# A state-space stage between gate products: the small products of a batch put in one run, VectorE's order written as a list, and weight tables multiplied out of PSUM

## The chip, the cores and the metric

The kernel runs on one core of a Trainium2 chip. The core has TensorE (PE, with a separate line PEld for loading weights), VectorE (DVE), ScalarE (ACT), GpSimd (POOL) and SyncE (SP), which issues transfers. Each engine takes its instructions in one fixed order and waits at the first one whose inputs or buffers are not ready. SBUF is the memory that the engines work from. PSUM, in eight banks, takes what PE writes; DVE and ACT read and write it too.

The metric is the time of one execution on the device, in microseconds (us). The kernel before took 1144.9 us as the median of three runs (1141.12, 1144.90 and 1145.05).

## The reference, cut to what matters

The program is a trunk of two layers on 1024 time steps of width 1024, all in float32. Layer 0 projects the input once and feeds three things: a diagonal complex state-space layer, retention, and two gates; layer 1 is a convolution module.

```python
proj = h @ w_in                          # u_s5, g_s5, q, k, v, g_ret
# state-space layer: 64 groups of 16 channels, 64 complex states each
bu  = einsum('tbgh,gnh->tbgn', u, bb)    # bb: complex, from a, dt, b
x_t = lb * x_{t-1} + bu_t                # lb = exp(dt * a), complex, per state
y_t = re(einsum('tbgn,ghn->tbgh', x_t, c)) + d * u_t
y_s5  = glu(gelu(y)) * silu(g_s5)
y_ret = retention(q, k, v) * silu(g_ret)
x = x + concat(y_s5, y_ret) @ w_out
```

The change touches the recurrence (bu, x_t, y_t) and the order in which it stands between the products for `g_s5` and `g_ret`.

## The kernel before, in words

Every large product is computed three times over 128x512 tiles, with the high and low parts of both operands: high weight by high input, high weight by low input, low weight by high input (`mm3`, L200 to L202). A weight block of 128x1024 is loaded as `wf`, cast by ACT to its high part `wh` (L189) and the rest `wl = wf - wh` is made by DVE or POOL (L190); for the gate blocks g9 to g23 it is DVE.

The stage concerned is the second part of `layer0_front`. It makes the 16 gate blocks g8 to g23. A gate block is two halves of 24 matmuls (`mm_g`), and each half is scaled by DVE out of its PSUM bank (`gt = mm_g * R`, L393), then passed through Silu by ACT (L394). Between the gate blocks stand the eight batches B = 0 to 7 of the state-space layer, 128 channels in each, one batch to every two gate blocks. A batch works on 8 time steps at once:

- POOL multiplies out tables from powers of `lb`: `Mr`, `Mi` (input side), `Tc`, `Ts` (a rotation that makes the recurrence real), `W3` (output side), in L766 to L768.
- `W2` holds the input weights. For B = 0 and 1 it is `Mr`, `Mi` turned by PE (L857) and copied by ACT (L859). From B = 2 on DVE makes it by six products (L806 to L811) from tables `PT`, `BT` that transfers lay out in SBUF.
- PE: `v` = `U` x `W2` into two PSUM banks (L868). PE also makes the direct response of the first 8 steps, `kp` (L902, L903); ACT copies 112 of its columns to `Kg` (L905), and DVE adds the term `d` in the other 16 (L906). PE turns `Kg` (L908, the tile is `kt`), ACT copies it out, a transfer stores it in `k_d` and another (L915) reads it back as the banded table `Wd`, which ACT copies to `W1` (L917).
- DVE, on the two banks of `v`: a rotation (L876 to L881), two scans (L883), the rotation back (L890 to L893) and the states `S` (L894, L895).
- PE: `y` = `U` x `W1` (L932) + `S` x `W3` (L938), which ACT copies out (L942).

`v`, `kp`, `kt`, `y` and, for B = 0 and 1, the turned `W2` share five PSUM banks in turn (`ps_aux`). The gate blocks have three of their own. A scheduler sets the order on every engine, from a simulated timeline; `chained` fixes the order of a group of instructions among themselves only, and `issue_after` puts one behind another. `y` of a batch is written in the code behind the gate block that follows the next batch's `v`.

Of the kernel before, what the change touches and what calls it, by code (L numbers as in the profile page):

```python
# [11 lines left out]
F32 = mybir.dt.float32  # L12
# [3 lines left out]
ALU = mybir.AluOpType  # L16
# [3 lines left out]
P = 128  # L20
# [18 lines left out]
LANES = 2  # L39

# [30 lines left out]
class Trunk:  # L71
# [148 lines left out]
    def run(self):  # L220
# [31 lines left out]
        with ExitStack() as mid:  # L252
            self.mid = self.pool("mid", 1, stack=mid)
            self.ps_aux = self.pool("ps_aux", 5, PSUM, stack=mid)
            with ExitStack() as st:
                self.layer0_front(st)
            with ExitStack() as st:
                self.retention(st)
        with ExitStack() as st:
            self.layer0_back_and_layer1(st)  # L260


    def layer0_front(self, st):
# [3 lines left out]
        early = ExitStack()  # L267
# [145 lines left out]
        self.s5_tab, self.s5_back, self.s5_last = {}, {}, None  # L413
        self.s5_turned()
        self.s5_tables(0)
# [353 lines left out]

    def s5_turned(self):  # L770
# [20 lines left out]
    def s5_w2(self, B):  # L791

        nc, v = self.nc, self.nc.vector
        (ptr, pti), (btr, bti) = ([self.big(f"{n}{c}_{B}", f"{n}{c}", 1) for c in "ri"] for n in ("PT", "BT"))
        dp, db = self.pt_d, self.bt_d

        with self.tc.issue_after(self.u_load.ins):
            for c, (pt, bt) in enumerate(((ptr, btr), (pti, bti))):
                nc.sync.dma_start(pt[:].rearrange("p q n -> p (q n)"),
                                  bass.AP(tensor=dp.tensor, offset=dp.offset + (c * 2 * P + 4 * B) * P,  # L800
                                          ap=[[32 * P, 8], [0, 16], [1, 4 * P]]))
                nc.sync.dma_start(bt[:].rearrange("p q n -> p (q n)"),
                                  bass.AP(tensor=db.tensor, offset=db.offset + (c * 4 * P + 4 * B) * P,
                                          ap=[[0, 8], [32 * P, 16], [1, 4 * P]]))
        w2r, w2i = (self.big(f"W2{nm}_{B}", f"W2{nm}", 1) for nm in "ri")
        v.tensor_tensor(w2r[:], ptr[:], btr[:], op=ALU.mult)  # L806
        v.tensor_tensor(w2i[:], ptr[:], bti[:], op=ALU.mult)
        v.tensor_tensor(ptr[:], pti[:], bti[:], op=ALU.mult)
        v.tensor_tensor(pti[:], pti[:], btr[:], op=ALU.mult)
        v.tensor_tensor(w2r[:], w2r[:], ptr[:], op=ALU.subtract)  # L810
        v.tensor_tensor(w2i[:], w2i[:], pti[:], op=ALU.add)  # L811
        return [w2r, w2i]

    def s5_tables(self, B):
# [25 lines left out]
        self.s5_tab[B] = Mr, Mi, W3, Tc, Ts, R8, self.s5_w2(B) if B > 1 else None  # L840

    def s5_states(self, B):
# [11 lines left out]
        for nm, M in (("r", Mr), ("i", Mi)) if first else ():  # L854
            ps = self.bank(f"w2{nm}_{B}")
# [7 lines left out]
        for c in range(2):  # L863
            ps = self.bank(f"v{c}_{B}")
            for q in range(4):
                for g2 in range(2):
                    r = slice(64 * g2, 64 * g2 + 64)
                    nc.tensor.matmul(ps[r, q * P:(q + 1) * P], W2[c][:, q, r], U[:, 2 * q + g2, :],  # L868
                                     start=True, stop=True)
            V.append(ps)  # L870
        fl = lambda t: t[:].rearrange("p q n -> p (q n)")
# [25 lines left out]


        kp = self.bank(f"kp_{B}")
        for q in range(4):  # L900
            o = kp[q * 32:(q + 1) * 32, :P]
            nc.tensor.matmul(o, self.cbr[:, q0 + q, :], Mr[:, q, :], start=True, stop=False)  # L902
            nc.tensor.matmul(o, self.cbni[:, q0 + q, :], Mi[:, q, :], start=False, stop=True)  # L903
        Kg = w.tile([P, P], F32, name=f"Kg_{B}", tag="Kg", bufs=1)
        nc.scalar.copy(Kg[:, 16:], kp[:, 16:P])  # L905
        v.tensor_tensor(Kg[:, :16], kp[:, :16], self.dd[:, B, :], op=ALU.add)  # L906
        kp = self.bank(f"kt_{B}")
        nc.tensor.transpose(kp[:, :P], Kg[:], self.ident[:])  # L908
        Kt = w.tile([P, P], F32, name=f"Kt_{B}", tag="Kg", bufs=1)
        nc.scalar.copy(Kt[:], kp[:, :P])  # L910

        nc.sync.dma_start(self.k_d[B, 112:], Kt[:])
        Wd = w.tile([P, 8, P], F32, name=f"Wd_{B}", tag="yb", bufs=1)
        kd = self.k_d[B]
        nc.sync.dma_start(Wd[:], bass.AP(tensor=kd.tensor, offset=kd.offset, ap=[[P, P], [16 * P, 8], [1, P]]))  # L915
        W1 = w.tile([P, 8, P], F32, name=f"W1_{B}", tag="W1", bufs=1)
        nc.scalar.copy(W1[:].rearrange("p g (i h) -> p i g h", i=8), Wd[:].rearrange("p i (g h) -> p i g h", g=8))  # L917
        self.s5_back[B] = U, W1, W3, S

    def s5_out(self, B):  # L920
# [5 lines left out]
        ps = [self.bank(f"y{g2}_{B}") for g2 in range(2)]  # L926
# [13 lines left out]
        self.chained(products())  # L940
        for g2 in range(2):
            nc.scalar.copy(yb[:].rearrange("p (q g) m -> p q g m", g=2)[:, :, g2, :],  # L942
# [984 lines left out]
```

## Time and profile before

| what | value |
| --- | --- |
| three runs | 1141.12, 1144.90, 1145.05 us; median 1144.9 |
| the profiled execution, its own time | 1149.41 us |
| its span, from the first instruction to the last | 1147.6 us |
| PE busy | 1125.1 us (98%), 6286 instructions |
| PEld busy | 984.8 us (86%) |
| DVE busy | 850.0 us (74%) |
| ACT busy | 489.0 us (43%) |
| POOL busy | 654.7 us (57%) |
| transfers | 261.45 MB, 228 GB/s in the mean |
| the stage of the eight batches | from about 95 to 323 us of the span |

A row of the timeline gives the start in us from the beginning of the span, the duration in us, the engine, the line, the operation, what it writes and from what, the shape, and a count. The idle time ahead of it stands in square brackets with what ended it. Matmuls overlap one another: the distance between two starts tells what one costs. A row of the waits gives the engine, the instruction that waited and the one that released it; then the idle time, how often, and the mean. A row of the groups gives busy time and mean ns, and behind a bar the idle time just before them. A row of the windows gives its stretch, the length, the busy time of PE, PEld, DVE, ACT and POOL with the number of instructions, the granted clock of PE (1.00 is full speed), the busy share of the DMA engines and GB/s.

### The profile page before, as it was taken

The page shows a single profiled execution, that of the slowest core. Times are in us where ns is not written, and L with a number is a line of the kernel's source. Part 1 is how long each engine was busy: PE and PEld are TensorE (multiplying, and loading weights), DVE is VectorE, ACT ScalarE, POOL GpSimd, SP SyncE. Part 2 cuts the span into 40 slices and gives each one's busy share as a digit, 9 for nine tenths or more (in the row PEclk, how much of TensorE's full clock was granted, in tenths as well). Part 3 has the DMA queues.
Part 4 walks back from the last instruction along what each step waited for, and adds up shares of the span by engine and source line. Part 5 has one row for each costly group of instructions (what it writes and reads, how often), then busy time and mean ns, then how long its engine had stood idle before and what let it go on. Part 6 is the DMA issues. An engine that isn't in the chain of part 4 may idle for free.

```text
span 1147.6 us, 17204 instructions
## 1 busy us (share of the span) xinstructions
PE 1125.1 (98%) x6286; PEld 984.8 (86%) x6286; DVE 850.0 (74%) x1464; ACT 489.0 (43%) x719; POOL 654.7 (57%) x448
## 2 busy tenths in 40 slices
PE   9999989999999999999999999999999999999897
PEld 7888878888888888989887888888888888888787
DVE  6975778887417569486669522599999899999844
ACT  6423222232223231323436423545545676444673
POOL 2059999998236355232575111589544568677563
PEclk9999999999999999999999999999999999999999
DMA  9344345555378766859998988665778655367865
GB/s 353 110 135 153 120 151 175 194 186 179 133 259 278 265 215 193 284 185 333 386 361 299 318 297 283 189 234 203 250 246 297 239 178 172 121 195 250 273 229 191
DMA packets 117636, 261.45 MB, mean 228 GB/s; under 512 B 10672, under 2 KB 42288, under 8 KB 116912
## 3 DMA queue, kind: packets, MB, share of 16 engines
q1 hardware_dynamic: 114096, 247.78, 64.2%
q10 hardware_dynamic: 3456, 12.58, 2.9%
q8 instruction: 49, 0.80, 0.3%
q14 instruction: 35, 0.29, 0.1%
HBM read 181.48 MB, written 74.65 MB: 223 GB/s over the span
## 4 chain that ended last, share of the span: by engine, by line
PE 36%; DVE 8%; DMA 5%; POOL 2%; issue 2%; ACT 1%; POOLq 0%; SPq 0%; DVEq 0%; ACTq 0%
DVE cv L1534 6%; PE mm_wo L201 5%; PE mm_wo L200 5%; PE mm_wo L202 5%; PE mm_b L201 2%; PE mm_b L202 2%; PE mm_b L200 2%; PE mm_a L202 2%; PE mm_a L201 2%; PE mm_a L200 2%; PE mm_oc L202 2%; PE mm_oc L201 1%; PE mm_oc L200 1%; DMA yn<-yn_d 1%; DMA yg<-gs_d 1%
## 5 line engine op out<-in xcount | busy, mean ns | idle before, releaser
L1534 DVE SCALAR_TENSOR_TENSOR cv<-u,convw,cv 128x512 f32<-128x512 f32 x398 | 273.0, 749 | 6.7 <-ACT cv L1513 4.8
L1507 POOL TENSOR_TENSOR tp<-tp,tp 128x512 f32<-128x512 f32 x64 | 83.0, 1298 | 34.2 <-ACT tp L1506 33.2
L200 PE MATMUL mm_g<-xh,wh_g 128*128 128x512 f32 x256 | 99.6, 389 | 0.0
L201 PE MATMUL mm_g<-xl,wh_g 128*128 128x512 f32 x256 | 97.8, 382 | 0.0
L202 PE MATMUL mm_g<-xh,wl_g 128*128 128x512 f32 x256 | 97.7, 382 | 0.0
L437 POOL TENSOR_TENSOR s1q<-s1q,s1q 128x512 f32<-128x512 f32 x12 | 17.6, 1467 | 81.3 <-ACT s1q L432 81.3
L1506 ACT ACTIVATE tp<-u,convw 128x512 f32<-128x512 f32 x64 | 45.4, 718 | 36.1 <-POOL tp L1507 35.3
L200 PEld LDWEIGHTS mm_g<-xh,wh_g 128*128 128x128 f32 x256 | 48.9, 191 | 8.7 <-issue 1.2
L202 PEld LDWEIGHTS mm_g<-xh,wl_g 128*128 128x128 f32 x256 | 48.7, 190 | 7.1
L201 PEld LDWEIGHTS mm_g<-xl,wh_g 128*128 128x128 f32 x256 | 48.8, 191 | 6.9 <-issue 0.4
L190 POOL TENSOR_TENSOR wl_glu<-wf_glu,wh_glu 128x1024 fp32r<-128x1024 f32 x14 | 34.0, 2428 | 30.9 <-ACT wh_glu L189 30.9
L201 PE MATMUL mm_oc<-zl,wh_woc 128*128 128x512 f32 (+1 forms) x144 | 51.6, 359 | 0.0
L200 PE MATMUL mm_oc<-zh,wh_woc 128*128 128x512 f32 (+1 forms) x144 | 51.6, 370 | 0.0
L202 PE MATMUL mm_oc<-zh,wl_woc 128*128 128x512 f32 (+1 forms) x144 | 51.3, 359 | 0.2 <-DMA wl_woc<-lo_woc 0.2
L190 POOL TENSOR_TENSOR wl_v<-wf_v,wh_v 128x1024 fp32r<-128x1024 f32 x12 | 30.7, 2559 | 35.2 <-ACT wh_v L189 35.2
L393 DVE TENSOR_TENSOR gt<-mm_g,R 128x512 f32<-128x512 f32 x32 | 21.8, 682 | 38.6 <-PE mm_g L202 38.6
L201 PE MATMUL mm_u<-xl,wh_u 128*128 128x512 f32 x128 | 48.4, 381 | 0.7 <-DVE xl L316 0.7
L200 PE MATMUL mm_wo<-ysh,wh_wos 128*128 128x512 f32 x128 | 48.9, 382 | 0.0
L200 PE MATMUL mm_g<-h1h,wh_cg 128*128 128x512 f32 x128 | 48.9, 382 | 0.0
L201 PE MATMUL mm_b<-h1l,wh_cb 128*128 128x512 f32 x128 | 48.7, 381 | 0.1
L202 PE MATMUL mm_b<-h1h,wl_cb 128*128 128x512 f32 x128 | 48.6, 380 | 0.0
L201 PE MATMUL mm_wo<-ysl,wh_wos 128*128 128x512 f32 x128 | 48.5, 379 | 0.0
(526 smaller groups left out, 3641.5 us busy)
## 6 DMA issues: line engine op xcount, KB each, us to landing
wf_g<-w_ab SPq DMA_DIRECT2D x16, 512.0 KB
wf_wos<-w_out SPq DMA_DIRECT2D x16, 512.0 KB
wf_wor<-w_out SPq DMA_DIRECT2D x16, 512.0 KB
wf_cb<-w_c SPq DMA_DIRECT2D x16, 512.0 KB
wf_ca<-w_c SPq DMA_DIRECT2D x16, 512.0 KB
wf_woc<-w_out_c SPq DMA_DIRECT2D x16, 512.0 KB
wf_v<-w_v SPq DMA_DIRECT2D x12, 512.0 KB
wf_cg<-w_c SPq DMA_DIRECT2D x11, 512.0 KB
```

What stands on the lines that cost most here:

```text
L190: self.low_made = lo[i].tensor_tensor(wl[:].rearrange(fl)[:, c], wf[:, c], h.bitcast(F32), op=ALU.subtract)
L200: nc.tensor.matmul(ps, wh[:, kb, :], xh, start=start, stop=False, **more)
L201: nc.tensor.matmul(ps, wh[:, kb, :], xl, start=False, stop=False, **more)
L202: self.last_mm = nc.tensor.matmul(ps, wl[:, kb, :], xh, start=False, stop=stop, **more)
L393: nc.vector.tensor_tensor(nat(gt[:, c]), un(ps[:]), nat(self.R[:, c]), op=ALU.mult)
L437: nc.gpsimd.tensor_tensor(a, a, sq[:], op=ALU.add)
L1506: nc.scalar.mul(sk[:], u[:, k:k + HALF], cw[:, nb, k:k + 1])
L1507: gp.tensor_tensor(s0[:], s0[:], sk[:], op=ALU.add)
L1534: v.scalar_tensor_tensor(dst[:], *tap, accs_[i][:], op0=ALU.mult, op1=ALU.add)
```

## The change

**One run a batch on PE.** `v`, `kp`, `y` of the batch before and the transpose of `Kg` are chained, so that they follow one another, and the gate block that comes next is placed behind the transpose. The two signs of `kp` are no longer alternated: four products of one, then four of the other.

**PSUM.** The five shared banks are closed once the tables are turned. Five banks with fixed names follow: `v0`, `v1`, `kp`, `y0`, `y1`. The transpose goes into columns 128 to 255 of the bank `kp`.

**W2.** For B = 1 it is now made by the six products as well. ACT copies the two `PT` tables into PSUM (`pw0`, `pw1`, in the banks of `y`), and each of the six products has one operand there.

**DVE's order.** A list gives DVE's order in the whole stage, each entry behind the one before. `Kg`, copied whole by DVE now, comes first in each batch, then the rotation, scans, rotation back and `S`, and then gates, `wl` and the six products for the next batch. For batch 0 the six products stand ahead of the rotation back.

**Smaller parts.** `Wd` has a buffer of its own (it shared that of `yb`), and `W1` is copied behind the copy of `yb`. A scratch size of the transfers is set to 1024.

```diff
+def s5_order():
+    seq = []
+    for b in range(8):
+        g, h = 8 + 2 * b, 9 + 2 * b
+        turns = [(f"m0_{b}", 0), (f"m1_{b}", 0)]
+        kern = [(f"Kg_{b}", 0), (f"Kg_{b}", 1)]
+        z = [(f"v{c}_{b}", n) for n in range(4) for c in range(2)]
...
+        seq += [*kern, *turns, *z[:6]]
+        if b:
+            seq += [*back, (f"gt_{g}", 0), (f"wl_g{h}", 0), *w[:3], (f"gt_{g}", 1), *w[3:]]
+        else:
+            seq += [(f"gt_{g}", 0), *w, *back, (f"gt_{g}", 1)]
+        seq += [(f"gt_{h}", 0), *([(f"wl_g{g + 2}", 0)] if b < 7 else []), (f"gt_{h}", 1)]
+    return [("PE", ("mm_g8_0", 6), ("v1_0", 7)),
+            *(("Activation", (f"pw0_{b + 1}", 0), (f"gt_{8 + 2 * b}", 0)) for b in range(1, 7)),
+            *(("DVE", late, early) for early, late in zip(seq, seq[1:]))]
...
         for nb in range(8, 24):
             B = (nb - 8) // 2
             if nb % 2 == 0:
                 self.s5_states(B)
-            gate_block(nb, self.wnext(f"g{nb}"), self.gs_d if nb < 16 else self.gr_d)
-            if nb % 2 == 0 and B:
-                self.s5_out(B - 1)
+                if B:
+                    self.s5_out(B - 1)
+                self.s5_scan(B)
+                self.s5_local(B)
+            w = self.wnext(f"g{nb}")
+            with self.tc.issue_after(self.s5_turn.ins) if nb % 2 == 0 and B else nullcontext():
+                gate_block(nb, w, self.gs_d if nb < 16 else self.gr_d)
...
-        v.tensor_tensor(w2r[:], ptr[:], btr[:], op=ALU.mult)
-        v.tensor_tensor(w2i[:], ptr[:], bti[:], op=ALU.mult)
-        v.tensor_tensor(ptr[:], pti[:], bti[:], op=ALU.mult)
-        v.tensor_tensor(pti[:], pti[:], btr[:], op=ALU.mult)
-        v.tensor_tensor(w2r[:], w2r[:], ptr[:], op=ALU.subtract)
-        v.tensor_tensor(w2i[:], w2i[:], pti[:], op=ALU.add)
+        for bank, t in ((pr, ptr), (pi, pti)):
+            nc.scalar.copy(bank[:], t[:].rearrange("p q n -> p (q n)"))
+        v.tensor_tensor(w2r, pr[:], br, op=ALU.mult)
+        v.tensor_tensor(w2i, pr[:], bi, op=ALU.mult)
+        v.tensor_tensor(pr[:], pi[:], bi, op=ALU.mult)
+        v.tensor_tensor(pi[:], pi[:], br, op=ALU.mult)
+        v.tensor_tensor(w2r, w2r, pr[:], op=ALU.subtract)
+        v.tensor_tensor(w2i, w2i, pi[:], op=ALU.add)
...
-        self.s5_tab[B] = Mr, Mi, W3, Tc, Ts, R8, self.s5_w2(B) if B > 1 else None
+        self.s5_tab[B] = Mr, Mi, W3, Tc, Ts, R8, self.s5_w2(B) if B else None
...
-        nc.scalar.copy(Kg[:, 16:], kp[:, 16:P])
+        v.tensor_copy(Kg[:, 16:], kp[:, 16:P])
         v.tensor_tensor(Kg[:, :16], kp[:, :16], self.dd[:, B, :], op=ALU.add)
...
-        kp = self.bank(f"kt_{B}")
-        nc.tensor.transpose(kp[:, :P], Kg[:], self.ident[:])
+        self.s5_turn = self.chained([nc.tensor.transpose(kp[:, P:2 * P], Kg[:], self.ident[:])], self.y_last)
...
-        Wd = w.tile([P, 8, P], F32, name=f"Wd_{B}", tag="yb", bufs=1)
+        Wd = w.tile([P, 8, P], F32, name=f"Wd_{B}", tag="Wd", bufs=1)
```

On PE, batch 2 stands so before, from the end of gate block g11 into g12. A name ends in the batch (or the block and its half) and a running number; the rows left out are matmuls of g12.

```order
L868 MATMUL v0_2_1623<-U_2_1621,W2r_2_1613 64x128 x8
L868 MATMUL v1_2_1632<-U_2_1621,W2i_2_1614 64x128 x8
L902 MATMUL kp_2_1661<-Mr_2_1571,s5_s5_cbr_485 32x128
L903 MATMUL kp_2_1661<-Mi_2_1572,s5_s5_cbi_487 32x128
...
L202 MATMUL mm_g12_1_1716<-xh_2_1_167,wl_g12_1419 128x512
L908 MATMUL kt_2_1673<-ident_69,Kg_2_1670 128x128
L200 MATMUL mm_g12_1_1716<-xh_3_1_180,wh_g12_1418 128x512
...
L202 MATMUL mm_g12_1_1716<-xh_7_1_220,wl_g12_1419 128x512
L932 MATMUL y0_1_1745<-U_1_1342,W1_1_1415 128x128
L932 MATMUL y1_1_1746<-U_1_1342,W1_1_1415 128x128
```

After the change the same place of PE reads so:

```order
L226 MATMUL mm_g11_1_1551<-xh_7_1_220,wl_g11_1251 128x512
L923 MATMUL v0_2_1635<-U_2_1633,W2r_2_1621 64x128 x8
L923 MATMUL v1_2_1644<-U_2_1633,W2i_2_1622 64x128 x8
L932 MATMUL kp_2_1653<-Mr_2_1579,s5_s5_cbr_485 32x128 x4
L934 MATMUL kp_2_1653<-Mi_2_1580,s5_s5_cbi_487 32x128 x4
L1003 MATMUL y0_1_1666<-U_1_1365,W1_1_1453 128x128
L1003 MATMUL y1_1_1667<-U_1_1365,W1_1_1453 128x128
...
L1009 MATMUL y1_1_1667<-S_1_1443,W3_1_1315 128x128
L947 MATMUL kp_2_1653<-ident_69,Kg_2_1662 128x128
L224 MATMUL mm_g12_0_1730<-xh_0_0_140,wh_g12_1456 128x512
```

The transpose of `Kg` and `y` of batch 1 have moved ahead of the whole of g12; before, 33 matmuls of g12 stood between `kp` and the transpose.

On DVE, the piece that leads to `Kg` of batch 2 reads so before:

```order
L393 TENSOR_TENSOR gt_11_1515<-mm_g11_1_1543,R0_354 128x512
L190 TENSOR_TENSOR wl_g14_1684<-wf_g14_1682,wh_g14_1683 128x1024
L806 TENSOR_TENSOR W2r_3_1878<-PTr_3_1870,BTr_3_1872 128x512
L876 TENSOR_TENSOR m0_2_1641<-v1_2_1632,Ts_2_1574 128x512
L877 TENSOR_TENSOR m1_2_1642<-v0_2_1623,Ts_2_1574 128x512
L878 TENSOR_TENSOR v0_2_1623<-v0_2_1623,Tc_2_1573 128x512
L879 TENSOR_TENSOR v1_2_1632<-v1_2_1632,Tc_2_1573 128x512
L807 TENSOR_TENSOR W2i_3_1879<-PTr_3_1870,BTi_3_1873 128x512
L906 TENSOR_TENSOR Kg_2_1670<-kp_2_1661,s5_s5_dd_489 128x16
L880 TENSOR_TENSOR v0_2_1623<-v0_2_1623,m0_2_1641 128x512
```

And so after the change:

```order
L866 TENSOR_TENSOR W2i_2_1622<-W2i_2_1622,pw1_2_1624 128x512
L435 TENSOR_TENSOR gt_11_1523<-mm_g11_0_1524,R0_354 128x512
L214 TENSOR_TENSOR wl_g12_1457<-wf_g12_1455,wh_g12_1456 128x1024
L435 TENSOR_TENSOR gt_11_1523<-mm_g11_1_1551,R0_354 128x512
L937 COPY Kg_2_1662<-kp_2_1653 128x112
L938 TENSOR_TENSOR Kg_2_1662<-kp_2_1653,s5_s5_dd_489 128x16
L959 TENSOR_TENSOR m0_2_1701<-v1_2_1644,Ts_2_1582 128x512
L960 TENSOR_TENSOR m1_2_1702<-v0_2_1635,Ts_2_1582 128x512
```

`Kg` stood behind `wl` of g14, two of the six products and four rotation products; now it is the first entry of the batch, with the second half's gate of g11 ahead of it. The products for batch 3 have moved behind `S` of batch 2.

In batch 0, DVE after the change goes on like this behind the two scans:

```order
L435 TENSOR_TENSOR gt_8_1193<-mm_g8_0_1194,R0_354 128x512
L861 TENSOR_TENSOR W2r_1_1353<-pw0_1_1355,BTr_1_1347 128x512
L862 TENSOR_TENSOR W2i_1_1354<-pw0_1_1355,BTi_1_1348 128x512
L863 TENSOR_TENSOR pw0_1_1355<-pw1_1_1356,BTi_1_1348 128x512
L864 TENSOR_TENSOR pw1_1_1356<-pw1_1_1356,BTr_1_1347 128x512
L865 TENSOR_TENSOR W2r_1_1353<-W2r_1_1353,pw0_1_1355 128x512
L866 TENSOR_TENSOR W2i_1_1354<-W2i_1_1354,pw1_1_1356 128x512
L973 TENSOR_TENSOR d0_0_1176<-v1_0_1138,Ts_0_1082 128x4x127
L974 TENSOR_TENSOR d1_0_1177<-v0_0_1129,Ts_0_1082 128x4x127
L975 TENSOR_TENSOR v0_0_1129<-v0_0_1129,Tc_0_1081 128x4x127
L976 TENSOR_TENSOR v1_0_1138<-v1_0_1138,Tc_0_1081 128x4x127
L977 TENSOR_TENSOR S_0_1175<-v0_0_1129,d0_0_1176 128x4x127
```

The six products are new for batch 1 and stand ahead of the rotation back of batch 0, whose last reader of the bank `v0` is the row of `S` at the end.

More of the change, by code (lines that the diff above doesn't have):

```diff
@@ L39 @@
 LANES = 2
+def s5_order():
[5 more added lines that the diff above has]
+        z = [(f"v{c}_{b}", n) for n in range(4) for c in range(2)]
+        back = [(f"d0_{b}", 0), (f"d1_{b}", 0), *z[6:], (f"S_{b}", 0), (f"S_{b}", 1)]
+        w = [(f"{t}_{b + 1}", n) for t, n in (("W2r", 0), ("W2i", 0), ("pw0", 0), ("pw1", 0), ("W2r", 1), ("W2i", 1))]
+        w = w if b < 7 else []
+        seq += [*kern, *turns, *z[:6]]
[7 more added lines that the diff above has]
+            *(("DVE", late, early) for early, late in zip(seq, seq[1:]))]
 def mv(ap):
@@ L260, in run, with order @@
             self.layer0_back_and_layer1(st)
+        self.order(s5_order())
+    def order(self, pairs):
+        seen, byname = {}, {}
+        for i in self.nc.cur_bb.bb.instructions:
+            if not i.outs:
+                continue
+            t = getattr(i.outs[0], "bass_ap", None)
+            if t is None:
+                continue
+            key = i.engine.name, t.tensor.name.rsplit("_", 1)[0]
+            n = seen[key] = seen.get(key, -1) + 1
+            byname[(*key, n)] = i
+        for engine, late, early in pairs:
+            self.tc.add_manual_dep(byname[(engine, *late)], byname[(engine, *early)].name, mybir.DependencyInfo(
+                mybir.DependencyClass.NoSync, mybir.DependencyReason.DATA), reason="order")
     def layer0_front(self, st):
@@ L896, in s5_states, with s5_local @@
         v.memset(S[:].rearrange("p c q m -> p (c q) m")[:, :, 0:1], 0.0)
[L899 to L904, printed above, removed]
-        nc.scalar.copy(Kg[:, 16:], kp[:, 16:P])
-        v.tensor_tensor(Kg[:, :16], kp[:, :16], self.dd[:, B, :], op=ALU.add)
-        kp = self.bank(f"kt_{B}")
[L908 to L912, printed above, removed]
-        Wd = w.tile([P, 8, P], F32, name=f"Wd_{B}", tag="yb", bufs=1)
[L914 to L917, printed above, removed]
+        self.s5_back[B] = U, Wd, W3, S
+    def s5_local(self, B):
+        U, Wd, W3, S = self.s5_back[B]
+        W1 = self.s5.tile([P, 8, P], F32, name=f"W1_{B}", tag="W1", bufs=1)
+        with self.tc.issue_after(self.yb_copy.ins) if B else nullcontext():
+            self.nc.scalar.copy(W1[:].rearrange("p g (i h) -> p i g h", i=8), Wd[:].rearrange("p i (g h) -> p i g h", g=8))
         self.s5_back[B] = U, W1, W3, S
@@ L925, in s5_out @@
         yb = self.s5.tile([P, 8, P], F32, name=f"yb_{B}", tag="yb", bufs=1)
-        ps = [self.bank(f"y{g2}_{B}") for g2 in range(2)]
+        ps = [self.s5_bank(f"y{g2}", B) for g2 in range(2)]
         cols = lambda q: slice(q * P, (q + 1) * P)
```

53 lines of the change are left out of this document (41 added, 12 removed).

## The prediction

> **What bounds the kernel now.** I read the page's busy times first, then PE's waits, then windows over single batches, and last the timelines of PE, DVE and ACT around the one wait that the change can reach.
>
> ```profile
> PE 1125.1 (98%) x6286; PEld 984.8 (86%) x6286; DVE 850.0 (74%) x1464; ACT 489.0 (43%) x719; POOL 654.7 (57%) x448
> PE kt L908 <- DVE Kg L906: 3.3, 1, 3.3
> ...
> PE mm_glu L200 <- DVE mm_gluz L1397: 2.6, 1, 2.6
> 236.66:264.14 27.48, 27.48 (x194) 23.98 (x193) 21.47 (x28) 8.22 (x16) 25.23 (x19) 1.00 0.56 183
> 162.08:165.50 3.42, 3.19 (x8) 2.62 (x9) 3.42 (x6) 0.00 (x0) 3.34 (x3) 0.50 0.00 0
> 1076.85:1080.27 3.42, 3.42 (x8) 2.10 (x7) 0.90 (x2) 2.57 (x5) 3.00 (x2) 0.50 0.99 356
> ```
>
> PE is busy 98% of the span, so only what PE does or waits for can move the time. The two rows of waits are the first and the last of the four that are 2.6 us or longer; only the first, `kt` behind `Kg`, lies in the stage that is changed. The first window is one undisturbed batch: 27.48 us, PE busy in all of it, DVE 21.47, ACT 8.22, POOL 25.23. The last two are the stretches just behind the first and the last of those waits: 3.42 us in which PE's granted clock is 0.50. Behind all four waits stands one. A wait of about 3 us so costs itself and then half of such a stretch.
>
> **The change, part by part.** First the wait.
>
> ```profile
> 149.16 1.09 PE L868 MATMUL v<-U,W2r 128*64 128x128 f32 x16
> 158.66 0.38 PE L202 MATMUL mm_g<-xh,wl_g 128*128 128x512 f32 x1
> 162.31 0.47 PE L908 MATMUL kt<-ident,Kg 128*128 128x128 f32 x1 [3.27 <-DVE Kg L906]
> 162.44 0.77 PE L200 MATMUL mm_g<-xh,wh_g 128*128 128x512 f32 x1
> 165.53 0.38 PE L201 MATMUL mm_g<-xl,wh_g 128*128 128x512 f32 x1
> 181.68 0.88 PE L868 MATMUL v<-U,W2r 128*64 128x128 f32 x12
> 140.26 0.41 SPq L915 DMA_DIRECT2D Wd<-k_d  x1
> 150.75 1.05 ACT L917 COPY W<-Wd 128x1024 f32<-128x1024 f32 x1 [10.23 <-DMA Wd<-k_d]
> 154.44 2.13 DVE L190 TENSOR_TENSOR wl_g<-wf_g,wh_g 128x1024 fp32r<-128x1024 f32 x1 [4.48 <-ACT wh_g L189]
> 156.50 1.77 DVE L806 TENSOR_TENSOR W2r<-PTr,BTr 128x512 f32<-128x512 f32 x1
> 162.10 0.16 DVE L906 TENSOR_TENSOR Kg<-kp,s_s_dd 128x16 f32<-128x16 f32 x1
> ```
>
> This is batch 2. The chain runs: the read of `Wd` is issued at 140.26; ACT's copy `W1` stands waiting 10.23 us for it and starts at 150.75; behind it ACT's cast `wh` is late, so DVE waits 4.48 us for `wl`; the products ahead of `Kg` are late with it, `Kg` comes at 162.10, and PE, which had 33 matmuls to run since `kp`, stands still. In the new order `Kg` is DVE's first work in a batch and needs nothing of ACT's; behind `kp` PE has the whole of `y` to run, and `W1` is waited for by nothing ahead of `Kg` of the same batch. So this wait goes.
>
> What it is worth: from 158.66 to 162.31 are 3.65 us where one big matmul needs 0.22 (below), so 3.43 lost. From 162.44 to 165.53 seven matmuls take 3.09 where 7 x 0.2157 = 1.51 would do; up to 0.1 of the 1.58 is the step out of a small product, so 1.5 is the clock. Check by the batch: 149.16 to 181.68 is 32.52, against 27.48 in the window, 5.04 more. **Term A: -5.0.** What is late next is nothing that the trace shows: the other batches have no wait.
>
> **Merging the small products.**
>
> ```profile
> 208.86 0.38 PE L202 MATMUL mm_g<-xh,wl_g 128*128 128x512 f32 x1
> 209.17 1.09 PE L868 MATMUL v<-U,W2r 128*64 128x128 f32 x16
> 211.66 0.48 PE L200 MATMUL mm_g<-xh,wh_g 128*128 128x512 f32 x1
> 211.98 0.38 PE L201 MATMUL mm_g<-xl,wh_g 128*128 128x512 f32 x1
> 218.67 0.38 PE L202 MATMUL mm_g<-xh,wl_g 128*128 128x512 f32 x1
> 222.24 1.95 PE L932 MATMUL y<-U,W 128*128 128x128 f32 x16
> 226.10 0.48 PE L200 MATMUL mm_g<-xh,wh_g 128*128 128x512 f32 x1
> 120.70 0.60 PE L857 MATMUL w2r<-ident,Mr 128*128 128x128 f32 x4
> 121.50 0.46 PE L200 MATMUL mm_g<-xh,wh_g 128*128 128x512 f32 x1
> ```
>
> From 211.98 to 218.67 are 31 steps of 0.2157. Going into small products costs 208.86 to 209.17, 0.31, so 0.09 more than a step; coming out costs 211.66 to 211.98, 0.32, so 0.10 more. Before, a batch has three runs, (`v`, `kp`), `kt` and `y`; after, one. The lone transpose costs the same wherever it stands. The exits behind `kp` and `y` fall away: 2 x 0.10 x 7 batches = 1.4. The turned `W2` of batch 1 takes 121.50 - 120.70 = 0.80 and an exit, 0.9; its six products go to DVE. Together 2.3. Not shown before are the joins inside the new run, `kp` to `y` and `y` to the transpose: no gain, since the work is the same, and at most what going in and out costs, 0.2 each, 14 x 0.2 = 2.8. I take nothing for them, as `v` and `kp` already follow each other without a step. **Term B: -2.3, between -2.3 and +0.5.**
>
> **DVE's order and the new wait.**
>
> ```profile
> 95.00 0.38 PE L786 MATMUL turn<-ident,s_pr 128*128 128x128 f32 x2
> 97.10 0.46 PE L200 MATMUL mm_g<-xh,wh_g 128*128 128x512 f32 x1
> 102.03 1.09 PE L868 MATMUL v<-U,W2r 128*64 128x128 f32 x16
> 103.92 0.45 PE L902 MATMUL kp<-Mr,s_s_cbr 128*32 128x128 f32 x8
> 104.11 0.69 DVE L876 TENSOR_TENSOR m<-v,Ts 128x512 f32<-128x512 f32 x1 [6.45 <-PE v L868]
> 104.72 0.68 DVE L877 TENSOR_TENSOR m<-v,Ts 128x512 f32<-128x512 f32 x1
> 108.39 2.33 DVE L883 TENSOR_TENSOR_SCAN v<-R,v 128x512 f32<-128x512 f32 x2
> L810 DVE TENSOR_TENSOR W2r<-W2r,PTr 128x512 f32<-128x512 f32 x4 | 7.3, 1824 | 0.0
> L811 DVE TENSOR_TENSOR W2i<-W2i,PTi 128x512 f32<-128x512 f32 x4 | 6.2, 1550 | 0.0
> L808 DVE TENSOR_TENSOR PTr<-PTi,BTi 128x512 f32<-128x512 f32 x4 | 6.1, 1515 | 0.0
> L807 DVE TENSOR_TENSOR W2i<-PTr,BTi 128x512 f32<-128x512 f32 x4 | 4.6, 1148 | 0.0
> L809 DVE TENSOR_TENSOR PTi<-PTi,BTr 128x512 f32<-128x512 f32 x4 | 3.8, 944 | 0.0
> L806 DVE TENSOR_TENSOR W2r<-PTr,BTr 128x512 f32<-128x512 f32 x4 | 3.6, 907 | 0.0
> L880 DVE TENSOR_TENSOR v<-v,m 128x512 f32<-128x512 f32 x5 | 3.4, 685 | 0.0
> ```
>
> The same product costs 0.685 with one operand in PSUM (L880; start to start 0.60, from 104.11 to 104.72 and on) and 0.91 to 1.82 with both in SBUF, 7.9 for the six, while POOL is busy 25 of 27.5 us. In PSUM I give the six 6 x 0.60 = 3.6, the row that they are nearest to; the other end is that they stay at 7.9. The Trainium skill, page "SBUF — State Buffer", section "Who interferes with whom", says that a VectorE instruction with two SBUF inputs contends with a GpSimd instruction that reads SBUF, and one with at most one SBUF input does not. By it the six would run at the PSUM price, and the rows agree; no run yet has shown these six so.
>
> For a steady batch that only widens the cover: DVE from 21.5 to about 17.5 us (copying 112 columns of `Kg` adds some 0.25, from ACT) in a batch of 27.3, ACT two copies of 0.6 more on 8.2, POOL as before. These cost nothing, since PE hides them. `Kg` would have to be done before PE has run `y`, 226.10 - 222.24 = 3.86 us; it takes about 0.5. That leaves 3.3. SP issues four more transfers (`PT`, `BT` of batch 1, at the 0.41 of the read of `Wd` 1.6 us of its time) where the DMA engines are busy 0.56 of the window; they are wanted at about 115, when DVE's scans are done, and I cost them at nothing. The store of `Kt` and the read of `Wd` follow the transpose as before, but with a whole batch, 27 us, until `y` wants them, against the 10.2 that the read took.
>
> Batch 0 is not steady. `v` of batch 1 writes the bank `v0`, which the first row of `S` of batch 0 reads last, and the list puts six products ahead of the rotation back. PE is there at 95.00 + 2.10 (all turned tiles, to 97.10) + 96 matmuls x 0.2157 = 20.71 + 2.49 for `v` and `kp` (209.17 to 211.66) + 0.3 for ins, outs and the transpose = 120.6. DVE: in the new order `kp` (0.60) and 38 big matmuls stand ahead of the end of `v`, which gives 95.00 + 2.10 + 8.20 + 0.60 + 1.90 + 0.2 = 108.0; DVE starts 0.19 later (103.92 to 104.11), 108.2. Six steps of 0.60, two scans 2.3, one gate 0.6, six products 3.6, four of the rotation back 2.4, one `S` 0.67: 121.4. **Term C: +0.7.** Its bounds: nothing, and, with the products at 7.9, 0.7 + 4.3 = 5.0. Behind PE here stands everything that is left.
>
> **Sum:** -5.0 - 2.3 + 0.7 = -6.6. Against the profiled execution, 1149.41, that is 1142.8. That execution lies 4.5 above the median of the runs, 1144.9; taken off the median it is **1138.3**.
>
> **The rivals.**
>
> Rival 1: the wait goes, but its half clock is not paid in a usual execution, or another wait pays one at another place. For it: the stretches are 3.42 us long whatever the wait. Against: four waits, four stretches. Then -5.0: 1139.9. The Trainium skill, page "TensorE: Matmul & The Clock Gate", section "Part 1: The HAM clock gate", has the clock watched in a free-running window of about 3.4 us and halved after an idle one. By it a wait shorter than the window need not always cost, so executions would differ by 1.5 us for each; the trace has waits of 2.6 to 3.3 that all did.
>
> Rival 2: the wait in batch 2 is the profiled execution's own. For it: 1149.41 against runs of 1141.12 to 1145.05, and a cause, a transfer landing 10 us after its issue, that can differ. Against: five terms of lateness ahead of it that stand in the program's order. Then only B and C remain, -1.6: 1143.3.
>
> Rival 3: the six products do not get cheaper out of PSUM. `v` of batch 1 then waits 5.0, which is above the 2.6 that was enough for a half clock: 4.3 + 1.5 more than forecast, 1144.1. For it: their other operand is a table that a transfer laid out, which no row shows against a PSUM bank. Against: L880 has a POOL table and a PSUM bank and costs 0.685.
>
> Rival 4, the slower side: DVE is late at `Kg`, and since `kp`, `y`, transpose and gate block are one chain, PE stands in each of 7 batches. The list allows DVE no passing: if `wl` of the block after next is late (a cast behind a transfer, as the 4.48 above), the second gate and `Kg` are late with it. Cover: 3.3 behind `kp`, 1.9 while `v` and `kp` run and the gate is done, and some 2 between the two gates, 7 in all. Each us beyond costs 7. Slower by 0.5% needs 1.75 us beyond the cover in each batch; at 2 it is 1138.3 + 14 = 1152.3. For it: a lateness of this kind did occur in batch 2. Against: only there, and 4.48 is under 7.
>
> **How the numbers follow.** The forecast has 0.45, with a range of its own from 1135.5 (one half clock less elsewhere) to 1141.1 (both joins of term B at their dear end); rival 1 0.12, rival 2 0.17, rival 3 0.12, rival 4 0.14. The range, 1135.0 to 1144.7, takes in all but rival 4 and the edges. Half a per cent of 1144.9 is 5.7 us, about what a measurement of this kernel can tell from no change; so faster begins below 1139.2 and slower above 1150.6. Of the forecast about seven tenths lie below 1139.2, of rival 1 some four tenths, of the others a little, and a larger gain than any of them, where timed executions of before pay more waits than this trace, adds some more: 0.43. Slower is rival 4 and what of rival 3 comes worse: 0.14. The rest, 0.43, is the same.
>
> **What would show it.** Right: no wait of `kt` in PE's waits; batches of 27.3 us from the start of one `v` to the next; a wait of under 1 us at `v` of batch 1; the six products near 0.69; DVE busy some 17 to 18 us a batch. Wrong: PE waiting at the transpose in several batches (rival 4), a wait of 3 us or more with a clock of 0.50 behind it at `v` of batch 1 (rival 3), joins of 0.1 or more between `kp` and `y`, or a stage that shrinks by 6 while something behind it, at the start of retention, grows by as much.

## The result, and the profile after

The changed kernel took 1142.62 us (median of 22 executions, 1139.53 to 1148.08), the kernel before 1144.94 in the same comparison (22 executions). The ratio is 0.9985 with a 95% interval from 0.9974 to 0.9996: 1.7 us faster, between 0.5 and 3.0. By the bound of 0.5% that is the same. The forecast was 1138.3.

The profiled execution took 1145.95, its span 1144.2 us. The lines that answer to those shown of before are, first, PE's waits of the changed kernel (the longest three, and the one in the stage):

```profile
PE ro L1294 <- DVE sc L1271: 4.1, 1, 4.1
PE cst L557 <- DVE cs L1689: 3.4, 1, 3.4
PE mm_glu L224 <- DVE mm_gluz L1470: 2.5, 1, 2.5
...
PE v L923 <- DVE S L977: 0.6, 1, 0.6
```

The transpose of `Kg` (now L947) no longer waits. The three long waits that are left lie in retention, in the GLU and in layer 1, all behind the stage.

PE's timeline shows the stage's first instruction, the wait of term C, batch 2 as one run, the start of batch 3, and the first matmul behind the stage:

```profile
94.86 0.38 PE L837 MATMUL turn<-ident,s_pr 128*128 128x128 f32 x2
...
120.48 0.38 PE L226 MATMUL mm_g<-xh,wl_g 128*128 128x512 f32 x1
121.50 1.09 PE L923 MATMUL v<-U,W2r 128*64 128x128 f32 x16 [0.65 <-DVE S L977]
...
148.92 1.09 PE L923 MATMUL v<-U,W2r 128*64 128x128 f32 x16
149.85 1.04 PE L923 MATMUL v<-U,W2i 128*64 128x128 f32 x16
150.82 0.42 PE L932 MATMUL kp<-Mr,s_s_cbr 128*32 128x128 f32 x8
151.06 0.40 PE L934 MATMUL kp<-Mi,s_s_cbi 128*32 128x128 f32 x8
151.40 2.05 PE L1003 MATMUL y<-U,W 128*128 128x128 f32 x16
153.38 2.06 PE L1009 MATMUL y<-S,W 64*128 64x128 f32 x32
155.36 0.33 PE L947 MATMUL kp<-ident,Kg 128*128 128x128 f32 x1
155.45 0.46 PE L224 MATMUL mm_g<-xh,wh_g 128*128 128x512 f32 x1
155.75 0.38 PE L225 MATMUL mm_g<-xl,wh_g 128*128 128x512 f32 x1
...
176.04 0.38 PE L226 MATMUL mm_g<-xh,wl_g 128*128 128x512 f32 x1
176.35 0.33 PE L923 MATMUL v<-U,W2r 128*64 128x128 f32 x2
...
317.23 0.48 PE L224 MATMUL mm_k<-xh,wh_k 128*128 128x512 f32 x1
```

A batch takes 176.35 - 148.92 = 27.43 us, where an undisturbed one took 27.48 before. The whole stage, from the first turned table to `mm_k`, takes 317.23 - 94.86 = 222.37. In the profile of before its end reads

```profile
322.89 0.48 PE L200 MATMUL mm_k<-xh,wh_k 128*128 128x512 f32 x1
```

which, from 95.00 on, is 227.89. So the two profiles show a stage that is 5.5 us shorter, near the forecast's 6.6. The timed executions show 1.7. That gap, 1.7 timed against 5.5 in the two profiles, is what the experiments are about.

DVE's groups (`wl`, then the dearest and the cheapest of the six products) and the window of one steady batch, after:

```profile
L214 DVE TENSOR_TENSOR wl_g<-wf_g,wh_g 128x1024 fp32r<-128x1024 f32 x9 | 17.8, 1973 | 0.0
L863 DVE TENSOR_TENSOR pw<-pw,BTi 128x512 f32<-128x512 f32 x4 | 2.8, 699 | 0.1
L862 DVE TENSOR_TENSOR W2i<-pw,BTi 128x512 f32<-128x512 f32 x4 | 2.7, 674 | 0.0
203.77:231.19 27.42, 27.42 (x194) 23.95 (x193) 20.24 (x29) 8.85 (x17) 23.71 (x18) 1.00 0.53 177
```

The six products take 0.67 to 0.70 each. DVE is busy 20.2 us in a batch, not 17.5: one reason is that `wl`, of which a batch has two and which still has both operands in SBUF, has gone up from 1.52 in the mean before to 1.97.

### The profile page after: what moved, and what is told of

Same layout as the page of the kernel before. It is cut to its first block, busy times and chain, and to the rows that moved or that the text cites. A ratio compares the mean times of both kernels' runs of the same rounds, so it can differ in the third digit from the quotient of the medians.

```text
span 1144.2 us, 17191 instructions
## 1 busy us (share of the span) xinstructions
PE 1122.5 (98%) x6278; PEld 983.6 (86%) x6278; DVE 833.1 (73%) x1478; ACT 492.6 (43%) x723; POOL 641.4 (56%) x448
## 4 chain that ended last, share of the span: by engine, by line
PE 63%; DVE 18%; DMA 10%; ACT 2%; issue 2%; POOL 2%; SPq 1%; POOLq 0%; DVEq 0%; ACTq 0%
DVE cv L1607 11%; PE mm_wo L224 5%; PE mm_wo L225 5%; PE mm_wo L226 5%; PE mm_g L224 4%; PE mm_g L225 4%; PE mm_g L226 4%; PE mm_u L226 2%; PE mm_u L224 2%; PE mm_u L225 2%; PE mm_oc L226 2%; PE mm_oc L225 1%; PE mm_oc L224 1%; PE y L1009 1%; PE y L1003 1%
```

## The experiments

Three theories stood at the start. Theory 1: the wait of batch 2 is in every execution of before, 5 us, and is paid in full. Theory 2: it belonged to the execution that was profiled. Theory 3: it is in every execution, but later waits (that of `ro`, in retention, had grown from 2.6 to 4.1 in the profile) take back what the stage gains. Theory 4 came out of the first runs: a wait here is paid in full, but in an ordinary execution it is much shorter than in the first profile.

Each ratio is to the kernel before on the same chip, with its 95% interval. Of the code, `...` stands for lines left out (in kg_first, late_kg and w1_behind a helper that sets the order of named instructions).

**The kernel before once more** (no edit).

> The kernel before, once more, with the granted clock of every timed execution. If the wait of the transpose for Kg in batch 2 is paid in every execution (theory 1), its profile shows a wait of about 3 us at the transpose again, with a clock of 0.50 behind it, and the mean clock of its executions lies 0.0015 below that of the changed kernel (one stretch of 3.42 us at half clock in 1142 us), whose executions had 0.994 to 0.998, mostly 0.996 or 0.997. If the wait belonged to the one execution that was profiled (theory 2), a new profile shows it shorter or not at all and the clocks are like those of the changed kernel.

1.0005 (0.9990 to 1.0019). Its profile, at 1143.88 us, has this at the same place (the timeline of PE, then of ACT):

```profile
161.39 0.33 PE L908 MATMUL kt<-ident,Kg 128*128 128x128 f32 x1 [1.95 <-DVE Kg L906]
...
150.32 1.04 ACT L917 COPY W<-Wd 128x1024 f32<-128x1024 f32 x1 [9.39 <-DMA Wd<-k_d]
```

and in its windows the clock ahead of and behind the transpose stays at 1.00:

```profile
158.30:161.70 3.40, 1.45 (x8) 0.96 (x7) 3.40 (x6) 0.00 (x0) 3.32 (x4) 1.00 0.19 76
161.70:165.10 3.40, 3.40 (x19) 3.00 (x18) 3.40 (x5) 0.00 (x0) 3.32 (x4) 1.00 0.00 0
```

The wait is there again, but it is 1.95 us, not 3.27, and there is no half clock behind it. Batch 2 takes 29.66, 2.17 more than 27.49, where the first profile had 5.03. Neither theory 1 nor theory 2 as written. The mean clocks of the timed executions do not decide it: 0.9951 for 35 executions of before in this comparison, against 0.9952 for kg_first and 0.9950 for s0_first below, which have no such wait; but 0.9945 for before against 0.9960 for after_again, in another.

**Kg ahead of the late wl, nothing else.** In the kernel before:

```diff
...
+        order(t, [("DVE", ("wl_g14", 0), ("Kg_2", 0))])
```

> The kernel before with one thing moved: on VectorE, wl of g14 stands behind Kg of batch 2 instead of ahead of it, so that Kg no longer waits for the late cast. The transpose then waits for nothing and batch 2 takes 27.5 us. Theory 1 (the wait is in every execution and what follows is rigid): 5.0 us faster than before, about 1140. Theory 2 (the wait is in few executions): within 1 us of before. Theory 3 (the wait is in every execution, but later waits take most of it back): 1.5 to 2.5 us faster, with later waits on PE that are longer by the difference.

0.9994 (0.9978 to 1.0011). PE no longer stops at the transpose:

```profile
158.00 0.27 PE L908 MATMUL kt<-ident,Kg 128*128 128x128 f32 x1
158.03 0.46 PE L201 MATMUL mm_g<-xl,wh_g 128*128 128x512 f32 x1
```

Batch 2 takes 27.49 and the stage 222.86, so that this one row of DVE's order gives all of the stage's gain but 0.49 us. And that with the read of `Wd` landing 10.56 us after its issue, later than in any profile of before. In time it is within 2.5 us faster and 1.3 slower: theory 1's 5.0 is outside.

**Work added in the stage.** In the changed kernel, 26 matmuls of 128x512 into a gate bank that nobody reads:

```diff
+            if nb == 15: self.s5_pad(w, xs)
...
```

> The changed kernel with 26 further matmuls of 128x512 between the gate blocks g15 and g16, into a gate bank that nobody reads: 26 x 0.2157 = 5.6 us more for PE in the stage, no wait and no change of the clock. Theories 1 and 2 (what follows the stage is rigid): 5.6 us slower than the changed kernel, 1148.2. Theory 3 (later waits swallow a shift of the stage): less, about 2.3, the gain that was measured for a stage 5.5 us shorter.

1.0024 (1.0007 to 1.0041), 2.7 us slower than before where the changed kernel was 1.7 faster: 4.5 us between the two, with some 2.3 either way. The stage is 227.98, 5.6 longer. By the middle values 4.5 of the 5.6 arrive at the end. Theory 3's 2.3 is at the edge of the interval, not excluded by this run alone.

**The rotation back ahead of the six products in batch 0.** In the changed kernel:

```diff
-            seq += [(f"gt_{g}", 0), *w, *back, (f"gt_{g}", 1)]
+            seq += [(f"gt_{g}", 0), *back, *w, (f"gt_{g}", 1)]
```

> The changed kernel with the rotation back and S of batch 0 ahead of the six products for batch 1 on VectorE. S of batch 0 is done some 3.6 us earlier, so the wait of v of batch 1 for the bank v0 goes: the stage is 0.7 us shorter in the profile (222.37 to 221.7 from the first turned tile to mm_k), as term C has it. In time 0.7 us, which is below what the executions can tell; if W2 of batch 1 comes too late instead, a wait of v for W2 stands there.

0.9997 (0.9982 to 1.0013); the stage is 222.36, as it was. The wait of `v` has changed its name only:

```profile
PE v L923 <- DVE W2r L865: 0.6, 1, 0.6
```

`v` of batch 1 needs `S` of batch 0 and `W2r`, and DVE has to do both, whichever comes first.

**Kg later still.** In the kernel before, one row of DVE moved, PE's order as it was:

```diff
...
+        order(t, [("DVE", ("Kg_2", 0), ("v1_2", 2)), ("PE", ("mm_g12_1", 9), ("kt_2", 0)), ("PE", ("mm_g13_0", 0), ("kt_2", 0))])
```

> The kernel before with one thing moved the other way: Kg of batch 2 stands on VectorE behind the two sums, the next product and the two scans too (1.2 + 1.4 + 2.3 = 4.9 us of work). The transpose keeps its place on PE and waits that much longer, about 7 us against the 2.0 of the last profile, and a stretch of half clock follows in every execution (1.5). Theory 3 (later waits swallow what the stage loses): about 2 us slower than before. Theory 4, that a wait here is paid in full and only the wait of the first profile was longer than a usual one: 4.9 + 1.5 = 6.4 slower than before, 1150.6.

1.0065 (1.0042 to 1.0087): 7.4 us slower, between 4.8 and 10. PE's timeline:

```profile
166.29 0.47 PE L908 MATMUL kt<-ident,Kg 128*128 128x128 f32 x1 [8.01 <-DVE Kg L906]
166.42 0.77 PE L200 MATMUL mm_g<-xh,wh_g 128*128 128x512 f32 x1
166.98 0.63 PE L201 MATMUL mm_g<-xl,wh_g 128*128 128x512 f32 x1
167.41 0.63 PE L202 MATMUL mm_g<-xh,wl_g 128*128 128x512 f32 x1
```

The wait is 8.0 us, and the matmuls behind it come 0.43 apart (166.98 to 167.41), half speed. Batch 2 takes 38.31, 10.8 more than 27.49. The kernel before already has some 1.6 of that in an ordinary execution (six profiles, below), so 9.2 were added in the stage and 7.4 arrived. Theory 3's 2 us is excluded. At least about half of what the stage loses is paid (4.8 of 9.2), and the interval takes in all of it.

**The changed kernel once more** (no edit).

> The changed kernel once more, beside the kernel before on the same chip. Theory 4: the stage takes 222.4 us again in the profile, since nothing in it waits for a transfer; the gain in time is that of the second profile of before, 225.03 - 222.37 = 2.7 us. Theory 1: 5.5.

0.9992 (0.9973 to 1.0012). The stage is 222.36 again: no wait in it followed a transfer's landing in either profile.

**Six profiles of before.** For the wait alone, besides before_again:

> A third profile of the kernel before, for the wait in batch 2 alone. Theory 4: the wait is again shorter than 3.3 us (about 2, from 1 to 3) and goes with the landing of the read of Wd of batch 1, which was 10.41 us after its issue in the first profile and 9.57 in the second; batch 2 takes 27.5 us and the wait, and 1.5 more only where a stretch of half clock follows. Theory 1: 32.5 us again.

> A fourth profile of the kernel before. Batch 2 took 32.52, 29.66 and 28.65 in the first three, with the read of Wd landing 10.41, 9.57 and 8.46 us after its issue. The timed runs (the changed kernel and its variants with a stage of 222.4 us lie 1.1 us under before) say that the wait of an ordinary execution is about 1 us, so that 28 to 29 is expected here, and 32.5 again if the first profile was the usual case.

> A fifth profile, as the fourth: batch 2 from 28 to 29 where the first profile was the exception, 32 and more where it was the rule; longer where Wd lands later.

> A sixth profile, as the fourth and the fifth: batch 2 from 28 to 29 where the first profile was the exception, 32 and more where it was the rule.

| profile of before | Wd lands after its issue, us | DVE from the start of wl to Kg, us | PE waits at kt, us | batch 2 above 27.49, us | stage, us |
| --- | --- | --- | --- | --- | --- |
| the one shown in the prediction | 10.41 | 7.65 | 3.27 | 5.03 | 227.89 |
| before_again | 9.57 | 7.17 | 1.95 | 2.17 | 225.03 |
| before_look2 | 8.46 | 7.38 | 0.95 | 1.16 | 224.02 |
| before_look3 | 8.78 | 7.03 | 1.03 | 1.25 | 224.11 |
| before_look4 | 10.21 | 6.53 | 1.92 | 2.13 | 224.99 |
| before_look5 | 8.51 | 7.30 | 1.03 | 1.25 | 224.11 |

The row of the wait in before_look2, and then that of before_look4 with DVE's `wl` and `Kg` ahead of it:

```profile
159.81 0.33 PE L908 MATMUL kt<-ident,Kg 128*128 128x128 f32 x1 [0.95 <-DVE Kg L906]
```

```profile
153.77 1.28 DVE L190 TENSOR_TENSOR wl_g<-wf_g,wh_g 128x1024 fp32r<-128x1024 f32 x1 [4.25 <-ACT wh_g L189]
160.30 0.16 DVE L906 TENSOR_TENSOR Kg<-kp,s_s_dd 128x16 f32<-128x16 f32 x1
160.52 0.33 PE L908 MATMUL kt<-ident,Kg 128*128 128x128 f32 x1 [1.92 <-DVE Kg L906]
```

The wait stands in all six, so theory 2 falls; it is 1 to 2 us in five of them, and only in the first did a stretch of half clock follow. These five executions took 1142.99 to 1145.47, about the median; the first took 1149.41. Without the first the stage of before is 224.45 in the mean. Against 222.37 after, that is 2.1 us, inside the measured 0.5 to 3.0. (With the first it is 2.7, inside too: the time alone does not tell the two apart.)

The landing is not all that sets the length. In before_look4 `Wd` landed only 0.20 us earlier than in the first profile, and the wait was 1.35 shorter: DVE needed 6.53 us from `wl` to `Kg` instead of 7.65, most of it in `wl` (1.28, against 2.13 in the prediction's row). `wl` and the two products in that stretch have both operands in SBUF; what that does to them is shown by w2_sbuf below.

Theory 3's reason falls by the same profiles: the wait of `ro` lies between 0.6 and 4.1 us in the six of before, so that 4.1 after the change is nothing new.

**The cause, by one copy on ACT.** In the kernel before, ACT's `W1` of batch 1 behind its cast for g14; PE's and DVE's orders are those of before:

```diff
...
+        order(t, [("Activation", ("W1_1", 0), ("wh_g14", 0))])
```

> The kernel before with ACT's copy W1 of batch 1 behind its cast for g14 instead of ahead of it; VectorE's and PE's orders are those of before. The profiles of before had the read of Wd land 8.46, 9.57 and 10.41 us after its issue, and batch 2 take 1.16, 2.17 and 5.03 us more than 27.49. If the landing is what makes Kg late (it holds up the copy, the cast behind it, wl and all of VectorE), batch 2 takes 27.49 here however late Wd lands. If VectorE's own load ahead of Kg is the cause, some wait of 1 us or more stays.

`Wd` landed 9.49 us after its issue, about as in before_again, and yet neither DVE nor PE waits (timelines of DVE and PE):

```profile
149.66 1.89 DVE L190 TENSOR_TENSOR wl_g<-wf_g,wh_g 128x1024 fp32r<-128x1024 f32 x1 [0.17 <-ACT wh_g L189]
156.81 0.16 DVE L906 TENSOR_TENSOR Kg<-kp,s_s_dd 128x16 f32<-128x16 f32 x1
...
158.41 0.27 PE L908 MATMUL kt<-ident,Kg 128*128 128x128 f32 x1
```

Batch 2 takes 27.49, and the whole execution, the only one, 1141.12 (before, on the same chip, 1140.15 to 1150.93). The chain of the prediction (landing, copy, cast, `wl`, products, `Kg`, transpose) is shown: moving its second link out of the queue removes the wait.

**The six products out of SBUF.** In the changed kernel, the same list for DVE, without ACT's two copies into PSUM:

```diff
-        for bank, t in ((pr, ptr), (pi, pti)):
-            nc.scalar.copy(bank[:], t[:].rearrange("p q n -> p (q n)"))
...
+        pr, pi, br, bi = fl(ptr), fl(pti), fl(btr), fl(bti)
...
```

> The changed kernel with the six products taking both operands from SBUF, as before, without ACT's two copies; the order of VectorE is the same list. If the second SBUF operand is what costs (a POOL that reads at the same time), the six take 0.9 to 1.8 us each again, 7.9 a batch instead of 4.1, and v of batch 1 waits some 4 us for S of batch 0 instead of 0.6; the other batches take 27.42 us as before, since VectorE has the cover. If the price came from where the products stood in the old order, they stay near 0.7.

It took 1154.51 in one execution, with a stage of 230.85, 8.5 longer than that of the changed kernel. The dearest and the cheapest of the six on DVE, `v` of batch 1 on PE, and a steady batch:

```profile
L858 DVE TENSOR_TENSOR W2r<-PTr,BTr 128x512 f32<-128x512 f32 x4 | 7.6, 1890 | 0.0
L861 DVE TENSOR_TENSOR PTi<-PTi,BTr 128x512 f32<-128x512 f32 x5 | 5.0, 993 | 0.0
...
127.93 1.98 PE L920 MATMUL v<-U,W2r 128*64 128x128 f32 x16 [7.01 <-DVE S L974]
...
204.00:231.42 27.42, 27.42 (x194) 23.95 (x193) 24.64 (x30) 7.97 (x14) 25.97 (x19) 1.00 0.54 175
```

The products are back at 0.99 to 1.89, so it is the second SBUF operand that costs, with POOL at work beside it, and not the place in the order. By the Trainium skill, page "SBUF — State Buffer", section "Who interferes with whom", such an instruction contends with GpSimd's reads, and POOL is busy 26 of 27.4 us here: the trace agrees. No run here took POOL's work away, but the profile of before has one form with POOL at work and without, in retention:

```profile
489.36 1.57 POOL L1078 TENSOR_TENSOR krot<-kraw,ropek 128x512 f32<-128x512 f32 x1 [6.58 <-DVE kraw L1065]
489.85 1.63 DVE L968 TENSOR_TENSOR yn<-yn,yn 128x512 f32<-128x512 f32 x1
492.61 0.68 DVE L969 TENSOR_TENSOR yn<-yn,yn 128x512 f32<-128x512 f32 x1
```

Both operands of `yn` lie in SBUF: 1.63 beside POOL's instruction, 0.68 with POOL idle.

The wait of `v` grew to 7.0, more than the 4 expected, and a half clock with it (the run of `v` takes twice its usual distance, 127.93 to 129.69). The steady batch stays at 27.42: there the price is hidden. So the move into PSUM is worth something in one place of the stage only, batch 0, and there only because the same list put six more products on DVE.

**y at the head of the run.** In the changed kernel:

```diff
+                if B:
+                    self.s5_out(B - 1)
                 self.s5_states(B)
-                if B:
-                    self.s5_out(B - 1)
...
```

> The changed kernel with y of the batch before at the head of the run: y, v, kp, transpose. The transpose then has nothing ahead of it while VectorE copies Kg, and waits some 0.2 + 0.25 + 0.1 + 0.1 = 0.65 us in each of batches 1 to 7. As for the joins: y behind a big matmul took 1.88 for its first 16 in the profile of before, and 1.98 behind kp in the changed kernel. If a change of the form of a matmul is what costs, y's first 16 go back to 1.88 here and the cost turns up at v and at the transpose; the batch is then 27.42 + 0.65, give or take 0.1. If it is the length of the run that counts, y stays at 1.98.

It took 1148.16 in one execution, with a stage of 228.53, 6.2 longer. PE in batch 2:

```profile
149.76 1.95 PE L1004 MATMUL y<-U,W 128*128 128x128 f32 x16
151.64 2.06 PE L1010 MATMUL y<-S,W 64*128 64x128 f32 x32
153.63 1.09 PE L924 MATMUL v<-U,W2r 128*64 128x128 f32 x16
...
156.65 0.33 PE L948 MATMUL kp<-ident,Kg 128*128 128x128 f32 x1 [0.48 <-DVE Kg L939]
```

The first 16 of `y` take 1.88 again (149.76 to 151.64), so the join behind `kp` was the 0.10, not the length of the run. The cost did not turn up at `v`, which takes 1.90 as ever. The batches are 28.4 us, 1.0 more: 0.48 at the transpose, which `y` no longer hides, and a second wait that was not expected, of gate matmuls for `wl`:

```profile
PE kp L948 <- DVE Kg L939: 3.4, 7, 0.5
...
PE mm_g L226 <- DVE wl_g L214: 2.8, 6, 0.7
```

That is rival 4 in small: in a fixed list, what is late once is late again.

**The products of batch 1 parted.** In the changed kernel:

```diff
-            seq += [(f"gt_{g}", 0), *w, *back, (f"gt_{g}", 1)]
+            seq += [(f"gt_{g}", 0), *w[:3], w[4], *back[:5], w[3], w[5], back[5], (f"gt_{g}", 1)]
```

> The changed kernel with the six products of batch 1 parted on VectorE: the four that W2r needs, then the rotation back and the first S of batch 0, then the other two and the second S. Both things that v of batch 1 waits for come 1.2 us earlier than the later of them now, so the wait of 0.6 goes and the stage takes 221.7 instead of 222.37, or up to 0.3 more where the second half of v waits for W2i. In time that is within what the executions can tell: 0 to 2 us below before, as the changed kernel.

0.9993 (0.9973 to 1.0013), and the stage 222.35. `v` starts 0.7 earlier and waits in its middle instead:

```profile
120.83 1.09 PE L923 MATMUL v<-U,W2r 128*64 128x128 f32 x16
122.42 1.09 PE L923 MATMUL v<-U,W2i 128*64 128x128 f32 x16 [0.49 <-DVE S L978]
```

The wait of term C is DVE's amount of work ahead of `v`: neither of the two other orders tried gains. No version beat the changed kernel by more than its measurement tells.

Four measurements have the same stage, 222.35 to 222.37: the changed kernel twice, s0_first and w2_split. Weighted by their intervals, their ratios 0.9985, 0.9992, 0.9997 and 0.9993 make 0.9990 (0.9982 to 0.9998), 1.1 us faster, between 0.3 and 2.0, where the stage is 2.1 shorter.

## Why the prediction was wrong

The direction and the main mechanisms held, the size did not: 1.7 us measured, 6.6 forecast. 1142.62 lies in the range that was given, 1135.0 to 1144.7, but not in the likeliest case's own.

- **Term A, "-5.0", is the step that failed.** The wait and its cause were read rightly, and it went. Its size was taken from one execution: 3.43 of wait and 1.5 of half clock. In the five other profiles batch 2 loses 1.16 to 2.17, 1.6 in the mean, with no half clock. In the one that was used `Wd` landed latest and DVE took longest behind it. The warning stood in the prediction: that execution lay 4.5 us above the median, and the chain began with a transfer's landing.
- **The sum was then taken off the median**, "taken off the median it is 1138.3". That takes 5.0 from an ordinary execution, which has 1.6 to lose there. Put against its own execution the sum was not far off in the stage (5.5 of 6.6).
- **Term B, "-2.3", was too much.** A steady batch gained 27.48 - 27.42 = 0.06, not 2 x 0.10 = 0.20. The text took nothing for the joins; `y` behind `kp` costs 0.10 (1.98 against 1.88 for 16) and the transpose behind `y` 0.09 (155.36 to 155.45) where it cost 0.03 between gate matmuls (158.00 to 158.03 in kg_first). The bound named for it, 0.2 each, holds both. The turned `W2` of batch 1 went as forecast, and what that gave, term C took.
- **Term C, "+0.7", was right.** DVE's `S` was forecast to end at 121.4, PE to arrive at 120.6; PE's `v` started at 121.50 after a wait of 0.65. The products at the PSUM price were right too, 0.67 to 0.70 against 0.69.
- **DVE's cover** was sized too well (20.2 busy, not 17.5; the rise of `wl` to 1.97 was not in the sum), with no consequence in the changed order. y_first shows what a thinner cover costs, 1.0 a batch.
- **Rival 1** was right on the half clock: in the five other profiles it is not paid. The prediction's "A wait of about 3 us so costs itself and then half of such a stretch" came from four waits of one execution (the stretch that it shows at 1076.85 lies behind the wait of `cst`, 2.9). It is no rule: in after_again the wait of `cst`, 2.73, left the clock at 1.00.
- **Rival 2**, the execution's own wait, was nearest in time, 1143.3, and half right in substance: most of the wait's length was that execution's own, though not the wait. It had 0.17.
- **Rival 3** did not come, and w2_sbuf shows what it would have cost: 7.0 at `v`, not 5.0. **Rival 4** did not come: `Kg` is in time in all batches.
- On the chances: "the same" had 0.43, as had "faster".

With the terms as measured, -1.6 for A, and -0.5 for everything else in the stage (222.86 in kg_first to 222.37), the sum is -2.1: 1142.8. With the 0.65 of term C, that -0.5 leaves some -1.1 for term B.

What stays open: whether retention takes back some of the gain. From `mm_k` to the first GLU product the six profiles of before take 209.4 to 213.8 us, 212.2 in the mean, and seven profiles of kernels with the changed order 212.2 to 215.8, 213.4 in the mean. The difference, 1.1, is of the size of the scatter, and no run here separates it. It would make up what lies between 2.1 in the stage and 1.1 in time, and the kernels that only move one row or copy of before (kg_first, w1_behind, late_kg: 208.8, 211.6 and 211.7) point the same way, but it is not shown. Nor did a run vary the smaller parts of the change by themselves, the scratch size and the buffer of `Wd` among them.

## What to carry to other kernels

A wait that begins with a transfer's landing and goes on through instructions of varying length has no fixed size: before a term is built on it, look at how far the profiled execution lies from the median, and take what lies above the median for that execution's own until a second profile shows it. Where a profile holds such a wait, the cheapest test of it is to move one instruction out of the queue between the landing and the wait; here one copy on ACT or one row on DVE gave all but 0.5 us of what the whole rewrite gave in the stage. Putting small products together saves only what the changes between their forms cost, and a new neighbour can cost as much as the old one.

## What was not expected of the hardware

- At the transpose, a wait of PE of 0.95 to 1.95 us left the clock at 1.00 (five profiles), one of 3.27 was followed by half clock for the rest of a stretch of 3.42, and one of 8.0 by half clock to 171.6, over 5 us. By the Trainium skill, page "TensorE: Matmul & The Clock Gate", section "Part 1: The HAM clock gate", the clock falls after an idle window of about 3.4 us; the trace agrees for the waits of 0.95 to 1.95 and for 8.0, and the 3.27 shows that somewhat less can do.
- Nor does the length of one wait decide by itself. In pad26 the wait of `ro` was 1.96 us, and a stretch at 0.50 followed; in after_again the wait of `cst` was 2.73, and the clock stayed at 1.00 (windows behind the two):

```profile
491.62:495.03 3.41, 3.41 (x19) 3.19 (x18) 3.41 (x12) 0.00 (x0) 0.00 (x0) 0.50 0.39 149
1069.70:1073.10 3.40, 3.33 (x10) 1.89 (x11) 2.44 (x4) 3.22 (x6) 2.43 (x2) 1.00 0.94 305
```

- The same read of the same 512 KB table, issued at the same place of the program, landed 8.46 to 10.41 us after its issue in six executions.
- 16 matmuls of `y` take 1.88 us behind a 128x512 matmul and 1.98 behind `kp`, whose rows read 128*32; `v` (128*64), 32 matmuls, takes 1.90 behind either a gate matmul or `y`.
